# Lambda's scratch in two 8 KB buffers instead of three, and x kept by halves of the features in a GLA / S5 trunk

## The chip, the core and the metric

The kernel runs on one core of one Trainium2 chip. The metric is the device time of one execution in microseconds. A core has five engines that run beside each other and wait for each other by semaphores: TensorE (PE in the profile; PEld are its weight loads), VectorE (DVE), ScalarE (ACT), GpSimd (POOL) and SyncE (SP), which here only issues DMA transfers, one after the other in its queue.

## The reference, cut to what matters

One sequence of 256 tokens with 2048 features goes through two layers: a chunked gated linear attention (GLA), then a complex-diagonal state-space layer (S5). Before each layer the input is modulated by a conditioning vector, after it stands a residual with LayerNorm.

```python
mod = einsum('bd,lde->lbe', silu(c), ada_w) + ada_b          # ada_w: 2 x 2048 x 6144
for i in range(2):
    shift, scale, gate = split(mod[i], 3)
    u = x * (1 + scale) + shift
    h = gla_mixer(u, ...) if i == 0 else s5_mixer(u, ...)
    x = layer_norm(ALPHA * x + (1 + gate) * h, ln_g[i], ln_b[i])
```

The first thing that the GLA layer does with `u` is the product with `gla_w_in` (queries, keys, values, the output gate z). The S5 layer needs numbers that depend on its weights alone. For 256 groups of 64 states:

```python
dt = exp(log_dt);  mag = exp(a_re * dt)
lb = mag * (cos(a_im * dt) + j sin(a_im * dt))               # Lambda
coef = ((lb - 1) * conj(a)) / (a_re**2 + a_im**2)            # scales b
```

The kernel needs `lb`, its powers 1 to 8, and `coef`. It calls this "Lambda's preparation".

## The kernel before, in words

Every large product is made at nearly f32 precision from two parts: a weight block of 256 x 512 is loaded (`wload`, L134, 512 KB, into a ring of four to six buffers), ScalarE makes its rounded part `hi` (`split`, L145), VectorE the remainder `lo` (L146), and TensorE multiplies the activations' parts with them, three matmuls for each pair (`mv_step`, L159, and `st_step`, L171). `hi` and `lo` have three buffers each.

The early part, up to some 360 us, works on values, queries and keys (tiles `v`, `q`, weights `wv`, `wq`). The 2048 features of `u` are taken in four blocks of 2, 2, 4 and 8 slices of 128 (`blocks`, L451), since a slice of `u` exists only when the conditioning (scale, shift) of these features does. `vqk_steps` (L382) gives the 12, 12, 24 and 48 steps of the blocks; the main loop (L801 to L823) runs them in order. Beside the steps run, by a table of steps (`put`, L768):

- the conditioning: `ada_pe` (L243) loads a block `a` of `ada_w` (L254, up to 1 MB), multiplies it on TensorE (`psa`, L275) or on VectorE (tile `row`, L265 to L267) and adds it to `mods`;
- x: `x_load` (L342) loads columns of x for both groups of 128 tokens, `u_tr` (L358) transposes them on TensorE (`psx`, L363), `u_fin` (L366) makes the two parts of `u`. The columns 0 to 255 are loaded ahead of the first step, 256 to 511 at step 0, 512 to 1023 at step 10, 1024 to 2047 at step 30. The last slices of the first half are transposed at step 23, those of the second half at steps 42 to 47;
- Lambda's preparation (`prep_lambda`, L500), a generator that the loop advances once in each step of the third block (steps 24 to 47) and empties after them. It works on tiles of 128 x 128 numbers on VectorE: an exponential by a polynomial (`expx`, L484), a reduction of the angle, two sines on ScalarE, `lr` and `li` (Lambda itself, the first rows of `pw`), `nr`, `den` and `coef` (`crci`), then the powers in three rounds that double their number (m = 1, 2, 4) with a scratch `tm`; last 64 small matmuls (`psl`, L591) on TensorE.

All tiles of up to 8 KB a partition that live longer, among them the blocks `a`, the rows of x, `u`, queries and keys, and Lambda's tiles, come from one pool of 12 buffers, `s8` (L49, `s8t`, L74). A tile gets a buffer when its first instruction comes up and gives it back after its last; an instruction whose buffer is not free waits, and whatever stands behind it in the queue of its engine waits too. In the early part `xrow0` and `xrow1` (one for each 128 tokens, all 2048 features) take two buffers from the first loads to the last transposes. Lambda takes three: `lamst` with 16 rows of 128 numbers, of which `new()` hands out one for each value, `pwr` for the powers, and `pwt` (4 KB used) for the scratch of the power rounds.

Which of the ready instructions stands first in an engine's queue is laid out by a planner when the program is built, from the order of the source, the dependencies and the free buffers. `tc.issue_after` keeps the TensorE and VectorE work of the table behind that of its step.

## Time and profile before

| | |
|---|---|
| median of 3 runs | 1847.61 us |
| lowest and highest run | 1844.9 and 1849.89 us |
| profiled execution, its own time | 1846.54 us |
| its span, first to last instruction | 1844.7 us |
| mean granted TensorE clock | 0.994 |
| TensorE busy | 1795.5 us (97%) |
| VectorE, ScalarE busy | 1422.5 us (77%), 897.4 us (49%) |
| HBM traffic | 432.81 MB read, 14.42 MB written |

A row of the profile names the line of the kernel, the engine, the operation, the tile written and the tiles read (buffer numbers left out), the shape, the count and the times. In the views by time the first number is the start in us from the first instruction, the second the duration; what stands in brackets is the idle time of the engine just before, and what ended it. In the views of waits there follow after the colon the total in us, the number of times and the longest. "issue" is time in which an engine waited for nothing that the profile shows. L136, L145, L146 and L510 are lines of helpers, so that there the tile's name tells what is meant.

### The profile page before, as it was taken

The numbers are of one execution on the slowest core, as the hardware profiler recorded it, in microseconds if no ns is written. First come the engines' busy times: TensorE is split into PE (matmuls) and PEld (weight loads), VectorE is DVE, ScalarE is ACT, GpSimd is POOL, SyncE is SP. The second block draws the span as 40 slices with busy tenths as digits, with TensorE's granted clock in tenths as the row PEclk, the third lists the DMA queues.
The fourth block names the chain that finished last, engine by engine and source line by source line (L and its number), as shares of the span: only waits on it lengthen the run. The fifth ranks groups of instructions, "written<-read, shape, count | busy, mean of one in ns | idle before, by whom it ended". The sixth has DMA issues, their size and how long they took to land.

```text
span 1844.7 us, 33886 instructions
## 1 busy us (share of the span) xinstructions
PE 1795.5 (97%) x13619; PEld 1588.5 (86%) x13619; DVE 1422.5 (77%) x1890; ACT 897.4 (49%) x1252; POOL 72.7 (4%) x78
## 2 busy tenths in 40 slices
PE   7999999999999999999999999999999999999997
PEld 5776897899999888899999999988888888888885
DVE  4877657879989888697899689888677775557556
ACT  5433557556556333654454454545544444444332
POOL 0000000000000000002223200000000000000000
PEclk9999999999999999999999999999999999999999
DMA  9996875889889998465654477899688886668653
GB/s 343 386 333 248 294 244 164 279 261 325 291 286 317 333 353 281 163 220 158 183 151 147 139 214 222 235 246 238 224 276 264 276 271 206 191 189 325 194 184 92
DMA packets 243798, 449.48 MB, mean 244 GB/s; under 512 B 19572, under 2 KB 48942, under 8 KB 242358
## 3 DMA queue, kind: packets, MB, share of 16 engines
q1 hardware_dynamic: 239320, 436.02, 73.9%
q0 software_dynamic: 3552, 10.24, 1.8%
q8 instruction: 107, 1.75, 0.4%
q10 hardware_dynamic: 768, 1.05, 0.2%
q14 instruction: 51, 0.42, 0.1%
HBM read 432.81 MB, written 14.42 MB: 242 GB/s over the span
## 4 chain that ended last, share of the span: by engine, by line
PE 86%; DVE 8%; DMA 3%; ACT 2%; issue 2%; SPq 0%; DVEq 0%; ACTq 0%
PE gl L192 13%; PE gl L193 7%; PE op L168 6%; PE op L167 6%; PE op L169 6%; PE z L182 3%; PE z L180 3%; PE z L181 3%; PE sz L180 3%; PE v L168 3%; PE v L169 3%; PE sz L181 3%; PE sz L182 3%; PE v L167 3%; PE su L180 2%; PE su L182 2%
## 5 line engine op out<-in xcount | busy, mean ns | idle before, releaser
L146 DVE TENSOR_TENSOR logl<-wgl,higl 128x1024 fp32r<-128x1024 f32 x128 | 156.5, 1224 | 115.3 <-ACT higl L145 113.7
L145 ACT CAST higl<-wgl 128x1024 fp32r<-128x1024 f32 x128 | 134.4, 1051 | 172.2 <-PE gl L192 167.9
L192 PE MATMUL gl<-yb,higl 128*128 128x512 f32 x512 | 179.6, 395 | 0.0
L192 PE MATMUL gl<-yp,higl 128*128 128x512 f32 x512 | 179.3, 395 | 0.1
L145 ACT CAST hio<-wo 128x1024 fp32r<-128x1024 f32 x95 | 100.2, 1055 | 155.3 <-PE op L169 127.3
L146 DVE TENSOR_TENSOR loo<-wo,hio 128x1024 fp32r<-128x1024 f32 x95 | 116.2, 1225 | 67.2 <-ACT hio L145 63.7
L315 DVE SCALAR_TENSOR_TENSOR acc<-wa,cs,acc 128x512 f32<-128x512 f32 x217 | 162.2, 748 | 4.8 <-DMA wa<-in_ada_w 2.1
L180 PE MATMUL su<-u1h,hisu 128*128 128x256 f32 x512 | 153.5, 301 | 1.9 <-DVE vv L1108 1.9
L180 PE MATMUL sz<-u1h,hisz 128*128 128x256 f32 x512 | 149.7, 292 | 1.2 <-ACT zs L1290 1.2
L180 PE MATMUL z<-u0h,hiz 128*128 128x256 f32 x512 | 148.7, 290 | 0.0
L182 PE MATMUL su<-u1h,losu 128*128 128x256 f32 x512 | 145.7, 286 | 0.4 <-DVE losu L146 0.4
L181 PE MATMUL su<-u1l,hisu 128*128 128x256 f32 x512 | 145.8, 285 | 0.0
L182 PE MATMUL z<-u0h,loz 128*128 128x256 f32 x512 | 144.9, 283 | 0.6 <-DVE loz L146 0.6
L182 PE MATMUL sz<-u1h,losz 128*128 128x256 f32 x512 | 144.9, 283 | 0.0
L181 PE MATMUL sz<-u1l,hisz 128*128 128x256 f32 x512 | 144.7, 283 | 0.0
L181 PE MATMUL z<-u0l,hiz 128*128 128x256 f32 x512 | 144.7, 283 | 0.0
L193 PE MATMUL gl<-yb,logl 128*128 128x256 f32 x512 | 143.4, 280 | 0.0
L193 PE MATMUL gl<-yp,logl 128*128 128x256 f32 x512 | 142.0, 280 | 0.0
L145 ACT CAST hisz<-wsz 128x1024 fp32r<-128x1024 f32 x64 | 66.9, 1051 | 107.2 <-PE sz L181 55.1
L192 PEld LDWEIGHTS gl<-yb,higl 128*128 128x128 f32 x512 | 96.0, 188 | 22.6
L192 PEld LDWEIGHTS gl<-yp,higl 128*128 128x128 f32 x512 | 95.8, 188 | 22.6 <-issue 0.6
L145 ACT CAST hisu<-wsu 128x1024 fp32r<-128x1024 f32 x64 | 66.7, 1050 | 95.1 <-PE su L181 70.6
(322 smaller groups left out, 5019.8 us busy)
## 6 DMA issues: line engine op xcount, KB each, us to landing
wgl<-in_s_w_glu SPq DMA_DIRECT2D x128, 512.0 KB, 4.7
wa<-in_ada_w SPq DMA_DIRECT2D x116, 512.0 KB, 5.1
wv<-in_gla_w_in SPq DMA_DIRECT2D x64, 512.0 KB, 6.1
wz<-in_gla_w_in SPq DMA_DIRECT2D x64, 512.0 KB, 5.2
wsu<-in_s_w_in SPq DMA_DIRECT2D x64, 512.0 KB, 3.7
wsz<-in_s_w_in SPq DMA_DIRECT2D x64, 512.0 KB, 4.3
wo<-in_s_w_out SPq DMA_DIRECT2D x64, 512.0 KB, 4.5
a<-in_ada_w SPq DMA_DIRECT2D x31, 1024.0 KB, 10.7
```

The costliest lines, as they stand in the source:

```text
L145: S.copy(hi, w)
L146: last_lo[0] = V.tensor_tensor(lo, w, hi.bitcast(F32), op=ALU.subtract).ins
L167: PE.matmul(banks[tt], lhsT=uh, rhs=hi[:, kk, :], start=(k == first), stop=False)
L168: PE.matmul(banks[tt], lhsT=uh, rhs=lo[:, kk, :], start=False, stop=False)
L169: last_mm[0] = PE.matmul(banks[tt], lhsT=ul, rhs=hi[:, kk, :], start=False, stop=(k == last)).ins
L180: PE.matmul(o, lhsT=wh, rhs=u.hi(k), start=(k == first), stop=False)
L181: PE.matmul(o, lhsT=wh, rhs=u.lo(k), start=False, stop=False)
L182: last_mm[0] = PE.matmul(o, lhsT=wl, rhs=u.hi(k), start=False, stop=(k == last)).ins
L192: PE.matmul(banks[f], lhsT=hi[:, kk, fs], rhs=u.both(k), start=(k == 0), stop=False)
L193: PE.matmul(banks[f][:, :T], lhsT=lo[:, kk, fs], rhs=u.hi(k), start=False, stop=(k == last))
L315: V.scalar_tensor_tensor(acc[0], w[:, kk, :], cs[:, k:k + 1], acc[0], op0=ALU.mult, op1=ALU.add)
```

## The change

x is kept in two tiles by halves of the features, 1024 for both token groups each; the second tile is asked for only when its columns are loaded, at step 30. In Lambda's preparation `pwt` goes, and its scratch lies in the rows 8 to 15 of `lamst`; the rows 0 to 6 serve several values in turn. `lamst` is so in use until the last power round.

| row of `lamst` | values, in turn |
|---|---|
| 0, 1 | `ar`, `ai` |
| 2 | `ag`, `cosm` |
| 3 | `mg`, `den` |
| 4 | `th`, `sn`, `t1` |
| 5 | `nn`, `sh`, `t2` |
| 6 | `r`, `nr` |

No arithmetic changes, and the number and shape of the transfers, transposes and VectorE instructions stay.

```diff
-    xr = []
+    xr = {}
     def x_load(c0, c1):
-        if not xr:
-            xr.extend([s8t(f"xrow{i}", [D]) for i in range(2)])
+        h = c0 // 1024
+        if h not in xr:
+            xr[h] = s8t(f"xrow{h}", [2, 1024])
         for tt in range(2):
-            dma(xr[tt][:, c0:c1], x[0, tt * P:(tt + 1) * P, c0:c1])
+            dma(xr[h][:, tt, c0 - 1024 * h:c1 - 1024 * h], x[0, tt * P:(tt + 1) * P, c0:c1])
...
-                PE.transpose(ps[:, kk * T + tt * P:kk * T + (tt + 1) * P], xr[tt][:, k * P:(k + 1) * P], ident)
+                PE.transpose(ps[:, kk * T + tt * P:kk * T + (tt + 1) * P], xr[k // 8][:, tt, k % 8 * P:(k % 8 + 1) * P], ident)
...
     def prep_lambda():
         st = s8t("lamst", [16, 128])
         pw = s8t("pwr", [8, 2, 128])
-        n_ = [0]
-        def new():
-            n_[0] += 1
-            return st[:, n_[0] - 1, :]
+        row = [st[:, i, :] for i in range(7)]
+        tm = st[:, 8:16, :].rearrange("g (a m) p -> g a m p", a=2)
...
-        ar, ai = new(), new()
+        ar, ai = row[0], row[1]
...
-        ag, mg, th = new(), new(), new()
+        ag, mg, th = row[2], row[3], row[4]
...
-        nn, r = new(), new()
+        nn, r = row[5], row[6]
...
-        sn, sh = new(), new()
+        sn, sh = row[4], row[5]
...
-        cosm = new()
+        cosm = row[2]
...
-        nr, den, t1, t2 = new(), new(), new(), new()
+        nr, den, t1, t2 = row[6], row[3], row[4], row[5]
...
-        tm = s8t("pwt", [2, 4, 128])
         for m in (1, 2, 4):
```

## The prediction

> **What bounds the kernel now.** I read the page first, then the windows of the stage in which the touched buffers live, then who waits for whom there, and last the timelines of VectorE, TensorE and the SP queue.

> ```profile
> span 1844.7 us, 33886 instructions
> PE 1795.5 (97%) x13619; PEld 1588.5 (86%) x13619; DVE 1422.5 (77%) x1890; ACT 897.4 (49%) x1252; POOL 72.7 (4%) x78
> PE 86%; DVE 8%; DMA 3%; ACT 2%; issue 2%; SPq 0%; DVEq 0%; ACTq 0%
> ```

> TensorE is busy 1795.5 of 1844.7 us: 49.2 us are idle in the whole program. None of its instructions is touched in number or shape, so a gain can only be a part of those 49.2 us, and of them only the part that falls where the change acts. The next view cuts the early stages; columns are the busy time of PE, weight loads, DVE, ACT and POOL, the granted clock, the DMA share and GB/s.

> ```profile
> 20.00:105.00 85.00, 80.69 (x475) 66.01 (x475) 65.19 (x100) 40.58 (x63) 0.00 (x0) 0.96 1.05 374
> 105.00:150.00 45.00, 43.45 (x230) 30.24 (x230) 33.97 (x87) 15.12 (x20) 0.00 (x0) 1.00 0.88 312
> 150.00:168.00 18.00, 14.07 (x125) 9.10 (x124) 17.61 (x38) 3.70 (x7) 0.00 (x0) 1.00 0.40 130
> 168.00:206.00 38.00, 38.00 (x308) 32.55 (x306) 24.55 (x43) 15.71 (x23) 0.00 (x0) 1.00 0.89 319
> 206.00:230.00 24.00, 22.14 (x183) 21.23 (x182) 15.18 (x20) 17.30 (x22) 4.04 (x4) 1.00 0.94 304
> ```

> The limits differ by stage. From 150 to 168 us VectorE is full (17.61 of 18.00), DMA is nearly empty (0.40) and PE loses 3.93 us; from 168 to 206 us PE loses nothing. The waits of PE and of the SP queue in this stretch:

> ```profile
> PE v L168 <- DVE lov L146: 3.8, 2, 1.9
> PE v L167 <- ACT hiv L145: 1.6, 1, 1.6
> PE pspw L610 <- ACT pd L603: 1.0, 1, 1.0
> PE pspw L610 <- ACT lc L612: 0.8, 2, 0.4
> SPq L254 <- PE psa L275: 29.4, 6, 9.3
> SPq L254 <- DVE crci L510: 9.7, 1, 9.7
> ```

> PE waits 7.2 us from 105 to 230 us, always for VectorE or ScalarE. The SP queue stands 39.1 us at L254, the load of a conditioning block `a`, until a buffer is given back: six times by the matmuls `psa` that read an older block, once by the end of Lambda's scratch `lamst`. That is the shortage the change relieves, and no PE wait of this list ends on a DMA.

> **The change, part by part.** *Buffers.* There are 12. Four are held in this stage by `u0h0`, `u0l0`, `qk0`, `qk1`; before, both `xrow` buffers are held until the last token transposes. Afterwards one half of x is enough until step 30, none is held between steps 23 and 30, and `pwt` needs none. The SP queue in the stage:

> ```profile
> 123.23 0.93 SPq L346 DMA_DIRECT2D xrow<-in_x  x2
> 133.66 0.37 SPq L254 DMA_DIRECT2D a<-in_ada_w  x1
> 135.47 2.25 SPq L136 DMA_DIRECT2D wv<-in_gla_w_in  x2
> 144.80 0.37 SPq L254 DMA_DIRECT2D a<-in_ada_w  x1
> 145.26 0.46 SPq L136 DMA_DIRECT2D wq<-in_gla_w_in  x1
> 155.48 0.37 SPq L254 DMA_DIRECT2D a<-in_ada_w  x1
> 155.90 1.01 SPq L136 DMA_DIRECT2D wq<-in_gla_w_in  x2
> 166.33 0.37 SPq L254 DMA_DIRECT2D a<-in_ada_w  x1
> ```

> With one or two buffers more, the `a` loads at 133.66, 144.80 and 155.48 can go right behind the load ahead of them: the second at about 137.8 (the end of the row at 135.47), the third as soon as an older block has been read, some us after that, and the first weight of the two at 155.90 follows at once. So most of the 39.1 us leave the SP queue. For the end of the kernel I take 0 from this. What hides the late loads now is the weights' lead: the rows at 151 to 168 us show PE short of casts and remainders that VectorE makes, not of data, and from 168 to 206 us PE is never idle. Bounds: from 0 down to the 7.2 us of all PE waits above; 0 is nearer, as none of the four rows ends on a DMA.

> *x by halves.* Eight loads remain eight, of the same bytes; 32 transposes remain 32 of one shape; the two loads at 123.23 wait for a new buffer instead of writing columns of an old one. Their data is read here:

> ```profile
> 181.91 0.60 PE L363 MATMUL psx<-ident,xrow 128*128 128x128 f32 x4
> 169.19 0.69 DVE L401 TENSOR_TENSOR vbig<-vbig,v 128x512 f32<-128x512 f32 x1 [1.35 <-PE v L169]
> ```

> 58 us later. Were the buffer late by the longest wait seen (9.3 us), the weights queued behind it would move by as much, which is the collision rival below; I take 0. `lamst` is now held to the end of the power loop (about 166.7 us instead of just before the load at 155.48 that got it), but with the freed buffers nobody asks for that one before the load that now leaves at 166.33: 0.

> *Rows used in turn.* Seven rows serve fourteen values. For most the order was forced by data already: `cosm`, `sn`, `sh`, `nr`, `t2` each overwrite a value whose last reader ran before their own inputs exist. One case differs: `den`, from `ar` and `ai` alone, now lies in the row of `mg`, and its helper `t1` in the row of `sn`; both are read by `lr` and `li`. VectorE's queue is laid out by a planner, and before the change it pulled those four instructions far forward:

> ```profile
> 121.99 0.81 DVE L510 TENSOR_TENSOR lamst<-lamst 128x128 f32<-128x128 f32 x3
> 122.84 0.95 DVE L557 RECIPROCAL lamst<-lamst 128x128 f32<-128x128 f32 x1
> 125.03 0.16 DVE L241 SCALAR_TENSOR_TENSOR mods<-psmod,abT 128x4 f32<-128x4 f32 x1 [1.23 <-PE psmod L236]
> ```

> They ran at 122 us, ahead of everything else of Lambda, in a pause: the next instruction waited 1.23 us for PE, so taking them away there gains nothing. They now come behind `lr` and `li`, here:

> ```profile
> 152.37 0.49 DVE L510 TENSOR_TENSOR pwr<-lamst 128x128 f32<-128x128 f32 x2
> 152.78 0.22 DVE L553 TENSOR_SCALAR lamst<-pwr 128x128 f32<-128x128 f32 x1
> 155.34 0.29 DVE L510 TENSOR_TENSOR pwt<-pwr 128x128 f32<-128x128 f32 x1
> 155.54 1.22 DVE L146 TENSOR_TENSOR lov<-wv,hiv 128x1024 fp32r<-128x1024 f32 x1
> 160.49 1.22 DVE L146 TENSOR_TENSOR lov<-wv,hiv 128x1024 fp32r<-128x1024 f32 x1
> 161.63 1.29 DVE L510 TENSOR_TENSOR pwt<-pwr 128x512 f32<-128x512 f32 x2
> 166.01 0.69 DVE L510 TENSOR_TENSOR pwr<-pwt 128x512 f32<-128x512 f32 x1
> 156.81 0.50 PE L168 MATMUL v<-lov,u0h 128*128 128x512 f32 x1 [1.89 <-DVE lov L146]
> 161.76 0.50 PE L168 MATMUL v<-lov,u0h 128*128 128x512 f32 x1 [1.94 <-DVE lov L146]
> 166.77 0.58 PE L591 MATMUL psl<-ident,pwr 128*32 128x32 f32 x32
> ```

> This is the stretch in which VectorE has no pause and PE waits for it twice. The four instructions took from 121.99 to 123.79, 1.80 us; back to back, each starts some 0.08 us before the end of the one ahead (0.29 long, 0.20 from 155.34 to 155.54), so they lengthen a full queue by about **1.7 us**. Queued behind them: the remainders `lov` at 155.54 and 160.49, for which PE waits, and the last power row at 166.01 + 0.69 = 166.70, at which PE arrives at 166.77. All three are on the path, so the 1.7 us are paid once. Bounds: 0, if the planner sets them behind the remainders and into the pause of 1.35 us at 169.19 (its row is above); and 1.7 us plus the power loop's tail, 166.70 - 161.63 = 5.1 us, if PE has to stand for it. I take 1.7, since the queue was laid out with Lambda ahead of the remainders.

> [...]

> **Sum.** 0 (buffers) + 0 (x) + 1.7 (`den`) on the profiled execution's own 1846.54 us (span 1844.7 and 1.8 around it) gives **1848.2 us**. The median of the runs, 1847.61, lies 1.1 above that execution, and the same step on it would read 1849.3. A measurement of this kernel tells about 0.3%, 5.5 us, from no change: my forecast is no measurable change.

> **The rivals.**

> *The buffers were the limit after all* (faster). For it: 39.1 us of SP waits, and DMA at 0.40 of its time where PE loses most. Against it: those PE waits end on VectorE and ScalarE. If late loads stand behind them, all four rows fall: 1846.5 - 7.2 = 1839.3 us. [...]

> *PE stands at `psl`* (slower). The 64 matmuls `psl` keep their place in PE's queue whatever happens to Lambda. If the planner lets the four late instructions push the power loop's tail behind the remainders, PE reaches `psl` and waits for that tail: 1.7 + 5.1 = 6.8 us, 1853.3 us. It decides as soon as the last power row is written after PE has done all that is queued ahead; before, that margin was 166.77 - 166.70 = 0.07 us, which speaks for it. Against: the other order needs a new plan, and PE's queue would be planned anew too.

> *The four instructions vanish in a pause* (nothing). They are placed behind the remainders, or PE's two waits swallow them: 1846.5 us. The same time results if the change does not do what it says, and the loads stay bound by weight buffers.

> *Loads collide* (a little slower). Loads pulled forward compete with weights:

> ```profile
> a<-in_ada_w SPq DMA_DIRECT2D x11, 1024.0 KB, 9.3
> wv<-in_gla_w_in SPq DMA_DIRECT2D x10, 512.0 KB, 7.7
> 154.51 1.05 ACT L145 CAST hiv<-wv 128x1024 fp32r<-128x1024 f32 x1 [2.07 <-PE v L169]
> ```

> At the 374 GB/s of a full DMA window 1 MB takes 2.8 us. The last weight `wv` (issued by 137.7, landed some 7.7 us later at 145.4) is cast at 154.51: 9.1 us to spare. Four loads ahead of it cost 11.2 us, 2.1 more than it has: 1846.5 + 1.7 + 2.1 = 1850.3 us. It bites from the fourth load on.

> **How the numbers follow.** Forecast 0.36, nothing 0.20, collision 0.08: together 0.64 within 0.3%. Buffers the limit 0.17, faster by over 0.3%. PE at `psl` 0.19, slower by over 0.3%. The range takes the slower case in whole and the faster one down to its foot, 1839.0 to 1855.0 us: beyond it are plans that I cannot work out, some 2 in 10. The forecast's own range is 1845 to 1851.

> **What would show it.** Right: the reciprocal at L557 runs after `lr` and `li`, past 150 us, not at 122; the waits of L254 for `psa` and `crci` shrink to under 15 us together, yet PE's waits from 105 to 230 us stay between 7 and 11 us; DMA has more than 0.40 from 150 to 168 us. Wrong: PE's waits for `lov` go away (buffers), `psl` gets a wait of its own (the slower rival), `hiv` ends a wait on a DMA (collision), or a difference of over 3 us arises past 230 us, where nothing is touched.

## The result and the profile after

| | before | after |
|---|---|---|
| median of 22 runs each, side by side | 1846.61 us | 1852.63 us |
| lowest and highest run | 1843.68 and 1851.98 us | 1848.35 and 1857.09 us |
| profiled execution, its own time | 1846.54 us | 1852.82 us |
| mean granted TensorE clock of that execution | 0.994 | 0.991 |

The ratio is 1.0028, with a 95% interval of 1.002 to 1.0036: about 5 us slower (the medians lie 6.0 us apart). The 0.3% that I called the limit lies inside the interval, no change lies outside it. The forecast was 1848.2 us; its wide range of 1839 to 1855 us holds the time, the forecast's own range of 1845 to 1851 us does not.

The page of after begins so; PE does the same 13619 matmuls, but is busy 3.4 us longer, and its idle time grows from 49.2 to 52.1 us:

```profile
span 1851.0 us, 33889 instructions
PE 1798.9 (97%) x13619; PEld 1589.1 (86%) x13619; DVE 1421.6 (77%) x1890; ACT 898.8 (49%) x1252; POOL 75.4 (4%) x78
```

The windows of the early stages of after, columns as before (us; PE, PEld, DVE, ACT, POOL; granted clock, DMA share, GB/s):

```profile
105.00:150.00 45.00, 43.45 (x235) 30.45 (x235) 33.42 (x87) 15.35 (x22) 0.00 (x0) 1.00 0.97 345
150.00:168.00 18.00, 11.75 (x41) 8.33 (x39) 15.65 (x38) 4.10 (x4) 0.00 (x0) 0.85 0.43 148
168.00:206.00 38.00, 38.00 (x330) 29.29 (x332) 22.86 (x37) 12.23 (x18) 0.00 (x0) 0.94 0.76 258
206.00:230.00 24.00, 22.92 (x187) 21.41 (x187) 13.06 (x24) 14.96 (x20) 2.89 (x3) 1.00 0.69 211
```

From 150 to 168 us PE is busy 11.75 us, not 14.07, and the clock, 1.00 throughout before, is 0.85 here and 0.94 in the next stage. The waits of PE from 105 to 230 us, and below them those of the SP queue at the `a` loads from 105 to 200 us (after the colon: us in total, times, longest):

```profile
PE v L168 <- DVE lov L146: 6.1, 2, 3.5
PE v L167 <- ACT hiv L145: 1.6, 1, 1.6
PE pspw L609 <- ACT lc L611: 0.4, 1, 0.4
```

and, of the SP queue:

```profile
SPq L254 <- PE psa L275: 15.1, 2, 13.5
SPq L254 <- PE v L169: 0.6, 1, 0.6
SPq L136 <- DVE lov L146: 24.4, 8, 6.2
```

The SP queue's 39.1 us for `psa` and `crci` have become 15.1 us, and the wait for `crci` is gone: the change does what it says. But the queue now stands longer at the weight loads (L136), 24.4 us for buffers that the remainders `lov` read (all its waits of this stretch sum to 73.5 us in both kernels), where the same view of before has:

```profile
SPq L136 <- DVE lov L146: 10.1, 4, 5.1
```

PE gains nothing by it; its two waits for `lov` rise from 3.8 to 6.1 us. The timelines show where, VectorE's first (start and duration in us):

```profile
153.58 0.49 DVE L510 TENSOR_TENSOR pwr<-lamst 128x128 f32<-128x128 f32 x2
155.12 0.95 DVE L557 RECIPROCAL lamst<-lamst 128x128 f32<-128x128 f32 x1
158.34 1.23 DVE L146 TENSOR_TENSOR lov<-wv,hiv 128x1024 fp32r<-128x1024 f32 x1
162.16 0.69 DVE L403 TENSOR_TENSOR vbig<-vbig,v 128x512 f32<-128x512 f32 x1 [0.67 <-PE v L169]
163.56 0.69 DVE L403 TENSOR_TENSOR vbig<-vbig,v 128x512 f32<-128x512 f32 x1 [0.38 <-PE v L169]
164.17 1.29 DVE L510 TENSOR_TENSOR lamst<-pwr 128x512 f32<-128x512 f32 x2
165.37 1.22 DVE L146 TENSOR_TENSOR lov<-wv,hiv 128x1024 fp32r<-128x1024 f32 x1
```

PE in the same time:

```profile
159.63 0.79 PE L168 MATMUL v<-lov,u0h 128*128 128x512 f32 x1 [3.49 <-DVE lov L146]
160.65 0.63 PE L167 MATMUL v<-hiv,u0h 128*128 128x512 f32 x1
166.64 0.80 PE L168 MATMUL v<-lov,u0h 128*128 128x512 f32 x1 [2.66 <-DVE lov L146]
177.71 0.28 PE L180 MATMUL q<-u0h,hiq 128*128 128x256 f32 x1
```

The reciprocal runs at 155.12 us behind `lr` and `li`, as forecast. The first wait grows by 3.49 - 1.89 = 1.60 us, about the 1.7 us of the four instructions. The second grows too, by 0.72 us. And behind each wait the matmuls are slow: 0.63 us long, where before they took 0.39. The first product with queries starts at 177.71 us; before, it started at 170.36. Of these 7.35 us, 1.2 were there already when `lr` and `li` ran (153.58 us against 152.37); about 6.1 arise here.

One more cut of the windows shows why. The clock's changes in the record lie on a comb with teeth 3.41 us apart (in after at 159.12, 162.53, 165.95 and, two teeth on, 172.77 us); cut on that comb, after reads:

```profile
155.71:159.12 3.41, 0.43 (x2) 0.00 (x1) 3.41 (x14) 1.05 (x1) 0.00 (x0) 1.00 0.96 362
159.12:162.53 3.41, 2.90 (x7) 2.32 (x8) 2.67 (x7) 0.00 (x0) 0.00 (x0) 0.50 0.49 145
162.53:165.95 3.42, 1.46 (x7) 0.85 (x5) 3.04 (x6) 1.05 (x1) 0.00 (x0) 1.00 0.02 8
165.95:169.36 3.41, 2.72 (x36) 1.86 (x37) 3.41 (x5) 0.00 (x0) 0.00 (x0) 0.50 0.00 0
169.36:172.77 3.41, 3.41 (x11) 1.86 (x13) 1.91 (x3) 0.00 (x0) 0.00 (x0) 0.50 0.02 5
```

In the interval behind one in which PE was mostly idle (0.43 of 3.41 us busy, 1.46 of 3.42), TensorE is here granted half its clock; a third interval at half clock follows one at half clock in which PE was busy for 2.72 us. The price can be read from PE's rows: from the end of the first wait to the first product with queries it takes 18.1 us (159.63 to 177.71), before 13.6 us (156.81 to 170.36). Of the 4.5 us more, 0.7 are the second wait and 3.8 the slow matmuls. With the first wait's 1.6 us these are the 6.1 us. The kernel before has the same two waits, shorter. These are its two emptiest intervals of this stretch, and the clock stays full in them and behind them:

```profile
153.18:156.58 3.40, 1.75 (x8) 1.13 (x6) 3.40 (x14) 1.05 (x1) 0.00 (x0) 1.00 0.02 2
160.01:163.42 3.41, 1.66 (x7) 1.39 (x8) 3.41 (x6) 0.45 (x1) 0.00 (x0) 1.00 0.83 295
```

So the theory was, ahead of the experiments: **A**, the late `den` makes PE wait longer for `lov`, and the longer waits cost clock. Its rivals: **B**, x by halves or the buffers it frees; **C**, the longer hold of `lamst` with the third buffer gone; and that the clock has nothing to do with the waits.

### The profile page after: what moved, and what is told of

Read it like the earlier page. It is cut to its first block, busy times and chain, and to the rows that moved or that the text cites. A ratio compares the mean times of both kernels' runs of the same rounds, so it can differ in the third digit from the quotient of the medians.

```text
span 1851.0 us, 33889 instructions
## 1 busy us (share of the span) xinstructions
PE 1798.9 (97%) x13619; PEld 1589.1 (86%) x13619; DVE 1421.6 (77%) x1890; ACT 898.8 (49%) x1252; POOL 75.4 (4%) x78
## 3 DMA queue, kind: packets, MB, share of 16 engines
q8 instruction: 107, 1.75, 0.4%
q10 hardware_dynamic: 768, 1.05, 0.2%
## 4 chain that ended last, share of the span: by engine, by line
PE 82%; DVE 10%; DMA 3%; issue 2%; ACT 2%; SPq 1%; DVEq 0%; ACTq 0%
PE gl L192 13%; PE gl L193 7%; PE op L168 6%; PE op L169 6%; PE op L167 6%; PE z L182 3%; PE z L180 3%; PE z L181 3%; PE v L168 3%; PE v L169 3%; PE v L167 3%; PE sz L180 2%; PE sz L182 2%; PE sz L181 2%; PE su L180 2%
## 5 line engine op out<-in xcount | busy, mean ns | idle before, releaser
L146 DVE TENSOR_TENSOR logl<-wgl,higl 128x1024 fp32r<-128x1024 f32 x128 | 156.5, 1224 | 114.4 <-ACT higl L145 112.5
L145 ACT CAST higl<-wgl 128x1024 fp32r<-128x1024 f32 x128 | 134.6, 1052 | 172.6 <-PE gl L192 163.4
L145 ACT CAST hio<-wo 128x1024 fp32r<-128x1024 f32 x95 | 100.3, 1056 | 154.1 <-PE op L169 130.5
L146 DVE TENSOR_TENSOR loo<-wo,hio 128x1024 fp32r<-128x1024 f32 x95 | 116.6, 1229 | 66.8 <-ACT hio L145 64.8
L145 ACT CAST hisz<-wsz 128x1024 fp32r<-128x1024 f32 x64 | 67.0, 1051 | 103.2 <-PE sz L181 55.3
L168 PE MATMUL v<-lov,u0h 128*128 128x512 f32 x256 | 104.4, 409 | 10.0 <-DVE lov L146 9.9
## 6 DMA issues: line engine op xcount, KB each, us to landing
wgl<-in_s_w_glu SPq DMA_DIRECT2D x128, 512.0 KB, 4.8
wa<-in_ada_w SPq DMA_DIRECT2D x116, 512.0 KB, 4.8
wv<-in_gla_w_in SPq DMA_DIRECT2D x64, 512.0 KB, 5.7
wz<-in_gla_w_in SPq DMA_DIRECT2D x64, 512.0 KB, 5.3
wsu<-in_s_w_in SPq DMA_DIRECT2D x64, 512.0 KB, 3.7
wsz<-in_s_w_in SPq DMA_DIRECT2D x64, 512.0 KB, 3.8
wo<-in_s_w_out SPq DMA_DIRECT2D x64, 512.0 KB, 4.5
a<-in_ada_w SPq DMA_DIRECT2D x31, 1024.0 KB, 10.8
```

The source lines that it names most:

```text
L145: S.copy(hi, w)
L146: last_lo[0] = V.tensor_tensor(lo, w, hi.bitcast(F32), op=ALU.subtract).ins
L168: PE.matmul(banks[tt], lhsT=uh, rhs=lo[:, kk, :], start=False, stop=False)
```

## The experiments

All were timed against the kernel before on the same chip. The table gives means. The four groups of one chip each (e1 to e4; e5 to e8; e9 and e10; e11 and e12) had runs of before beside them, with means of 1847.3, 1847.6, 1847.0 and 1847.2 us. "Clock" is one minus the mean granted clock (noted to 0.001 for each run), times the span, averaged over the runs (its standard error is 0.3 to 0.6 us in each row); "rest" is the time less that. "Clock" counts all the time at half clock, whether TensorE worked in it or not.

| kernel | runs | mean us | ratio to before, 95% interval | clock, us | rest, us |
|---|---|---|---|---|---|
| before (the runs beside the first four) | 35 | 1847.3 | | 14.2 | 1833.1 |
| after | 22 | 1852.2 | 1.0028 (1.002 to 1.0036) | 16.4 | 1835.8 |
| e1: after, `den` in rows of its own | 12 | 1847.4 | 0.9997 (0.9985 to 1.0009) | 13.7 | 1833.7 |
| e2: before, `den` in shared rows | 12 | 1851.2 | 1.0024 (1.0011 to 1.0036) | 16.8 | 1834.4 |
| e3: before, x by halves of the features | 12 | 1846.4 | 0.999 (0.9975 to 1.0005) | 13.4 | 1833.1 |
| e4: before, Lambda's part of the change | 12 | 1853.2 | 1.0032 (1.002 to 1.0045) | 17.0 | 1836.3 |
| e7: after, PE's waits filled | 12 | 1848.0 | 1.0001 (0.999 to 1.0012) | 12.2 | 1835.8 |
| e8: after, `den` computed twice | 12 | 1848.7 | 1.0007 (0.9996 to 1.0017) | 14.3 | 1834.3 |
| e10: before, PE's waits filled | 11 | 1847.3 | 0.9999 (0.9986 to 1.0012) | 12.9 | 1834.4 |
| e5: e1, Lambda six steps earlier | 12 | 1843.0 | 0.9977 (0.9965 to 0.9988) | 12.7 | 1830.3 |
| e6: after, Lambda six steps earlier | 9 | 1841.9 | 0.9968 (0.9955 to 0.998) | 12.3 | 1829.7 |
| e9: before, Lambda six steps earlier | 12 | 1845.1 | 0.9993 (0.9982 to 1.0005) | 13.1 | 1832.0 |
| e11: e6 again, beside e12 | 11 | 1844.4 | 0.9989 (0.9978 to 0.9999) | 13.1 | 1831.4 |
| e12: e9 again, beside e11 | 11 | 1844.8 | 0.9987 (0.9975 to 0.9999) | 12.6 | 1832.2 |

### Which part of the change

e1, on after:

```diff
-        row = [st[:, i, :] for i in range(7)]
+        row = [st[:, i, :] for i in range(8)]
...
-        nr, den, t1, t2 = row[6], row[3], row[4], row[5]
+        nr, den, t1, t2 = row[6], row[7], row[4], row[5]
+        dh = tm[:, 1, 3, :]
...
-        tt(t1, ai, ai, ALU.mult)
-        tt(den, den, t1, ALU.add)
+        tt(dh, ai, ai, ALU.mult)
+        tt(den, den, dh, ALU.add)
```

> The kernel after, but `den` lies in the free row 7 of `lamst` and its helper in row 15 (the last row of the power loop's scratch, not used before m = 4); two buffers, x by halves, the rest as in after. Theory A (late `den`): the four instructions run at about 122 us again, PE's waits for `lov` in 150-170 us fall from 6.2 to about 3.8 us, no half-clock interval in 150-175 us, time as before, about 1846.6 us (1845 to 1848.5). Theory B (x by halves or the buffers it frees is the cause): as after, about 1852.6 us, whatever `den` does. Theory C (the longer hold of `lamst` and the missing third buffer): as after, about 1852.6 us.

e2, on before:

```diff
-        nr, den, t1, t2 = new(), new(), new(), new()
+        nr, den, t1, t2 = new(), mg, sn, new()
```

> The kernel before, but `den` in the row of `mg` and `t1` in the row of `sn`; three buffers, all other rows their own, x by tokens. Theory A: reciprocal at about 155 us behind `lr` and `li`, PE's waits for `lov` in 150-170 us about 6 us, half-clock intervals of 3 to 10 us behind them, time as after, about 1852.6 us (1850.5 to 1854). Theory B: as before, 1846.6 us, as x is as before. Theory C: as before, 1846.6 us, as the three buffers are as before; the late `den` alone then costs at most the 1.7 us of its four instructions, 1848.3.

e3 is before with only the `x_load` and `u_tr` part of the change, e4 before with only its `prep_lambda`.

> The kernel before with only x kept by halves of the features; Lambda's preparation as before, in three buffers with rows of their own. Theory A: as before, 1846.6 us (1845 to 1848.5), the reciprocal at about 122 us, the SP queue's waits for `psa` shorter than 29.4 us all the same. Theory B: as after, about 1852.6 us. Theory C: as before, 1846.6 us.

> The kernel before with only Lambda's preparation as in after (two buffers, rows in turn); x kept by halves of the tokens. Theory A: as after, about 1852.6 us (1850.5 to 1854), reciprocal at about 155 us, waits for `lov` about 6 us, half-clock intervals behind them. Theory B: as before, 1846.6 us. Theory C: as after, 1852.6 us.

The two kernels with shared rows are slow, the two without are not, whatever x and the buffers do. One line of e2 (three buffers, x by tokens) already makes 3.9 us of loss, where after has 4.9; the intervals overlap. And e1, which has both freed buffers, x by halves and the longer hold of `lamst`, is as fast as before. B and C fall. In e1 the reciprocal (VectorE's timeline) and the two waits of PE (its waits from 105 to 230 us) are back where before has them:

```profile
123.54 0.95 DVE L558 RECIPROCAL lamst<-lamst 128x128 f32<-128x128 f32 x1
```

```profile
PE v L168 <- DVE lov L146: 3.7, 2, 1.9
```

and in the same view of waits e2 is as after:

```profile
PE v L168 <- DVE lov L146: 6.1, 2, 3.5
```

I had missed one thing of e1: there should have been no half-clock interval, and its profiled execution has two, with waits no longer than those of before:

```profile
154.37:157.79 3.42, 1.54 (x7) 1.00 (x6) 3.38 (x13) 1.05 (x1) 0.00 (x0) 1.00 1.01 369
157.79:161.20 3.41, 3.41 (x9) 2.64 (x9) 2.45 (x6) 0.00 (x0) 0.00 (x0) 0.50 0.68 217
161.20:164.61 3.41, 1.63 (x7) 1.01 (x7) 2.92 (x6) 1.05 (x1) 0.00 (x0) 1.00 0.00 0
164.61:168.03 3.42, 3.42 (x10) 2.63 (x9) 3.38 (x5) 0.00 (x0) 0.00 (x0) 0.50 0.00 0
```

The comb lies otherwise against the same waits and catches 1.54 and 1.63 busy us, where it caught 1.75 and 1.66 in before. So by these four intervals a wait of 1.9 us stands at the edge: whether it costs clock seems to depend on where the comb falls.

### Whether the clock follows the waits

e7, on after; in the steps of weights v63 and v72 twelve matmuls are put behind the first matmul with `hiv`, in `mv_step`. The weight tile `zp` is zero, so they add nothing. The heart of the edit, cut to it (the matmuls with `lov` are kept behind the last of them):

```diff
...
+                if fill and tt == 0 and kk == 0:
+                    for _ in range(fill):
+                        with tc.issue_after(m_):
+                            m_ = PE.matmul(banks[tt], lhsT=zp, rhs=hi[:, kk, :], start=False, stop=False).ins
...
```

> The kernel after, plus 24 extra matmuls on PE, twelve behind the first matmul with `hiv` of weight v63 and twelve behind that of v72, ahead of the first matmuls with `lov`: 128x512 with a weight tile of zeros, so that they add nothing to the bank. At 0.227 us each at full clock they take 2.7 us inside each of the two waits (3.49 and 2.66 us) and add no wait. Clock theory (PE left idle for most of a 3.4 us interval runs the next at half clock): the granted clock stays 1.0 from 150 to 180 us, and the two waits for `lov` end as early as in after; the mean falls by the clock's part of the loss, 2 to 3 us, to about 1849.5 us (after was 1852.2 in the mean), though PE has 24 matmuls more. Rival (the half clock has nothing to do with the idle time, or the late `lov` alone is the loss): no gain or, where the fill makes PE late, up to 1 us slower, 1852 to 1853.

The 24 matmuls more make the kernel 4.3 us faster than after (1848.0 against 1852.2). All of it is clock: the rest is 1835.8 us in both, the clock falls from 16.4 to 12.2 us. The comb's intervals in e7:

```profile
155.25:158.66 3.41, 3.41 (x17) 2.83 (x16) 3.41 (x15) 1.06 (x1) 0.00 (x0) 1.00 1.04 384
158.66:162.07 3.41, 2.64 (x12) 1.87 (x11) 3.34 (x8) 0.00 (x0) 0.00 (x0) 1.00 0.42 108
162.07:165.49 3.42, 3.42 (x16) 2.65 (x15) 3.42 (x6) 1.05 (x1) 0.00 (x0) 1.00 0.25 95
```

This shows cause, not company: PE was kept busy with work worth nothing, and the half clock went. VectorE's timeline of e7 also explains the second wait:

```profile
158.66 1.22 DVE L146 TENSOR_TENSOR lov<-wv,hiv 128x1024 fp32r<-128x1024 f32 x1
161.73 0.68 DVE L411 TENSOR_TENSOR vbig<-vbig,v 128x512 f32<-128x512 f32 x1
163.26 1.29 DVE L518 TENSOR_TENSOR lamst<-pwr 128x512 f32<-128x512 f32 x2
164.46 1.22 DVE L146 TENSOR_TENSOR lov<-wv,hiv 128x1024 fp32r<-128x1024 f32 x1
```

From one `lov` to the next it takes 5.80 us; in after 7.03 us, since there VectorE itself waited 0.67 and 0.38 us for PE at half clock, with the next `lov` behind; in before 4.95 us, since there the pair of 1.29 us stood behind the second `lov`, not ahead of it. So the new order puts the next `lov` 0.85 us later, and the slow clock another 1.2 us. But PE's own matmuls between its two waits take longer at half clock, too: 4.35 us in after against 3.01 in before. The two about cancel, and the wait itself grows by the order alone. The profile of e4 bears this out: its clock was full between the two waits, and they are about as long as in after:

```profile
159.24 0.50 PE L168 MATMUL v<-lov,u0h 128*128 128x512 f32 x1 [3.49 <-DVE lov L146]
165.04 0.79 PE L168 MATMUL v<-lov,u0h 128*128 128x512 f32 x1 [2.78 <-DVE lov L146]
```

e10 fills before's two waits in the same way, with seven matmuls each:

> The kernel before, plus seven extra matmuls with a weight tile of zeros (7 x 0.227 = 1.6 us) inside each of PE's two waits of 1.9 us for `lov`. Clock theory: the kernel before stands at the edge, its two waits leave an interval 0.45 to 0.53 busy, so that in some executions they cost half-clock intervals; the fill takes these away: mean clock loss 12 to 13 us in place of 14.1, mean time 1845.5 to 1846.5, and no half-clock interval from 150 to 175 us. Rival (waits of 1.9 us never cost clock): no change, 1847.4 us in the mean.

This did not settle it. The clock's part was 12.9 us (14.0 in the runs of before beside it), a difference of less than two of its standard errors; no half-clock interval lies in the stretch, but none does in the profile of before either. And the time did not fall, 1847.3 against 1847.0 us: the waits, fill included, got longer.

```profile
PE v L176 <- DVE lov L146: 1.8, 2, 1.3
```

That is the same view of e10's waits: 1.8 us, and 14 x 0.227 = 3.2 us of fill make 5.0 us, where before waits 3.8. The fill shifted VectorE's queue: the pair of 1.29 us now stands ahead of the second `lov`, as in after, and from one `lov` to the next it takes 6.13 us, where before takes 4.95. So whether waits of 1.9 us cost before any clock in the mean stays open.

### Twice the cost

e8, on after: the four lines of `den` written a second time behind the first, the same values again.

> The kernel after, with the four instructions of `den` written twice behind each other (the second time writes the same values again), so 1.7 us more on VectorE behind `lr` and `li`. Theory A with my price: PE's waits for `lov` grow by 1.7 us at the first of the two remainders, 6.2 to about 7.9 us, and the time by 1.7 us plus up to one more half-clock interval (1.7): about 1854 to 1856 us in the mean. Rival (it was only the new order in PE's and VectorE's queues that cost time): no growth, 1852.2.

A miss: not 1.7 us slower than after, but 3.6 us faster (1848.7). Its wait from 105 to 230 us, three rows of VectorE's timeline and two intervals of the comb say why:

```profile
PE v L168 <- DVE lov L146: 5.3, 1, 5.3
```

```profile
159.94 1.22 DVE L146 TENSOR_TENSOR lov<-wv,hiv 128x1024 fp32r<-128x1024 f32 x1
161.41 1.22 DVE L146 TENSOR_TENSOR lov<-wv,hiv 128x1024 fp32r<-128x1024 f32 x1
163.22 1.22 DVE L146 TENSOR_TENSOR lov<-wv,hiv 128x1024 fp32r<-128x1024 f32 x1
```

```profile
157.55:160.97 3.42, 0.00 (x0) 0.00 (x0) 3.42 (x12) 0.00 (x0) 0.00 (x0) 1.00 0.24 93
160.97:164.38 3.41, 3.16 (x8) 2.49 (x9) 3.41 (x7) 0.00 (x0) 0.00 (x0) 0.50 0.50 153
```

The first wait did grow, by 5.34 - 3.49 = 1.85 us, as priced. But the planner laid the queue out anew and put the next two `lov` at 161.41 and 163.22 us, ahead of most of the power loop; the second wait is gone, and one interval at half clock stands where after had three. One wait of 5.3 us was cheaper than two of 3.5 and 2.7. The rival that I set against my price (the order costs, too) has a part in it: VectorE's extra time is paid at the next remainder, and what is paid at the one after depends on the order. My price so holds for the first wait only; the time does not follow the number of late instructions.

### Taking the cause away

e5 (on e1), e6 (on after) and e9 (on before) advance Lambda's preparation from step 18 on, not 24, into the stretch in which VectorE had 11 us free:

```diff
-            if n == 2:
+            if n == 2 or n == 1 and i >= 6:
                 next(lam, None)
```

> The first experiment's kernel (`den` and its helper in rows of their own, otherwise as after), with the generator of Lambda's preparation advanced from the seventh weight step of the second block on, six steps earlier. Theory A (VectorE is full only from 150 to 168 us and has 11 us free from 105 to 150): the waits for `lov` in 150-170 us (3.7 us) go, no wait as long comes up before 150 us, no half-clock interval there; 3.7 us less and up to 2 us of clock: 1842 to 1844 us in the mean, faster than before. Rival (VectorE is short over the whole stretch, so the waits only move): `lov` waits of about the same sum at 115 to 150 us, time 1846 to 1848.

> The kernel after, rows shared as they are, with the generator advanced six steps earlier as in the run beside it. Theory A: the row sharing costs only where VectorE is full, so the time is that of the run beside it within 1 us, 1842 to 1845 us. Rival (the order that the shared rows force costs by itself): 2 us or more slower than the run beside it.

> The kernel before (three buffers, rows of their own, x by tokens) with the generator of Lambda's preparation advanced six weight steps earlier. Theory A (only VectorE's full stretch counts, buffers and x do not): the same gain as with the shared rows and halves of the features, 1842 to 1843.5 us in the mean. Rival (the freed buffers are what the earlier Lambda needs, as its `lamst` and `pwr` are held longer): the SP queue's waits for `psa` grow beyond 39 us and the gain is smaller, 1844.5 us or more.

e5 and e6 are faster than before, and within 1.1 us of each other: the shared rows cost nothing that these runs show once Lambda's chain runs where VectorE has time. The windows of e6 from 105 to 150 and from 150 to 180 us, where VectorE is now busy 41.43 of 45 and 14.49 of 30 us, and PE's waits for `lov` from 105 to 230 us:

```profile
105.00:150.00 45.00, 42.34 (x283) 28.46 (x282) 41.43 (x109) 14.84 (x22) 0.00 (x0) 1.00 0.89 309
150.00:180.00 30.00, 29.89 (x189) 23.62 (x188) 14.49 (x20) 9.98 (x11) 0.00 (x0) 1.00 0.89 324
```

```profile
PE v L168 <- DVE lov L146: 2.5, 2, 2.1
```

The waits for `lov` in the old place are gone; 2.5 us stand at 108 and 142 us. e5's own expectation missed in one point: it has a wait of 2.3 us for `hiv` ahead of 150 us, longer than any that went. In e11 and e12 an interval near 106 us, busy for 0.39 and 0.42, is followed by half clock. So the earlier Lambda, too, can cost clock, at a place of its own. e9 gained less (0.9993, the interval across 1), as its rival had it, but its SP queue did not wait longer for `psa` (26.1 us, not over 39), so that rival's reason was not seen. e11 and e12 set the two side by side on one chip:

> The kernel after with Lambda's preparation six steps earlier, once more, now on the same chip as its counterpart without the change. If the freed buffers are worth nothing even then, the two means lie within 1.5 us of each other, at 1842 to 1845.5 us. If the freed buffers are worth something once VectorE is out of the way, this one is faster by 2 to 3 us, as the separate runs (1841.9 against 1845.1 us) have it.

> The kernel before with Lambda's preparation six steps earlier, once more, on the same chip as the run beside it. Buffers worth nothing: within 1.5 us of it. Buffers worth something: slower than it by 2 to 3 us.

1844.4 and 1844.8 us: no difference beyond the noise (up to some 2 us would not show). The freed buffers show no worth here either. The gain of the kernel with the change over before was 5.7 us in the first comparison (e6) and 2.7 us in the second (e11): its sign is settled, its size is not. Against after it is 7 us or more in both, so the kernel with the change and an earlier Lambda beats both kernels.

## Why the prediction was right or wrong

**Buffers, 0; x by halves, 0.** Right. e1 (0.9997) has both freed buffers, e3 (0.999) that of x, each with the interval across 1, and e11 against e12 repeats it with VectorE out of the way. It fits the reason given, that none of PE's waits in this stage ended on a transfer. The waits of L254 for `psa` and `crci` fell to 15.1 us, where I had set under 15; the weight loads behind them took up the freed time as waits of their own.

**`den`, 1.7 us.** The mechanism was right, and the size at its place too (1.60 us). The step that failed is "all three are on the path, so the 1.7 us are paid once". They are paid once at the first `lov`; the third, the last power row, was never waited for. And the sum lacked two terms. The second wait grew by 0.72 us, from the new order (0.84 us in e4, whose clock was full there). And the clock: 2.2 us in the mean (16.4 against the 14.2 of the 35 runs in the table), 3.8 us in the profiled execution. With 2.7 us in the rest (the two waits, 1.60 + 0.72 = 2.3 us, are most of it) this makes the 4.9 us between those means; against the 22 runs of before beside it, whose clock was not noted run by run, after is 5.2 us slower. The part of the sum that was mis-sized is thus "1.7", which measured 4.9 to 5.2; I had read the clock's 1.00 in that stage as given, not as something which a longer wait takes away. VectorE does 1890 instructions in both kernels; where four of them stand was worth 3.9 us in e2 and this much in after.

**"PE stands at `psl`"** said 1853.3 us, the number nearest to the result, by a mechanism that did not occur: `psl` has no wait, its halves only stand later in PE's queue:

```profile
168.22 0.66 PE L590 MATMUL psl<-ident,pwr 128*32 128x32 f32 x32
174.69 0.46 PE L590 MATMUL psl<-ident,pwr 128*32 128x32 f32 x32
```

The prediction said that `psl` keeps its place in PE's queue whatever happens to Lambda; it did not. A number that fits shows no cause; e1 and e2 do. **"Four instructions vanish in a pause"** fell with the reciprocal at 155.12 us, **"Loads collide"** with `hiv`, whose only wait of PE is the 1.6 us of before, **"Buffers were the limit"** with e1 and e3.

**Chances and signs.** By the ratio the result is within 0.3%, the case that had 0.64, but only by 0.0002; by the medians it is just outside, on the side that had 0.19. That the 0.3% holds it is luck, and that the wide range holds it says little, since that range was drawn around nearly all the rivals; the forecast's own range, 1845 to 1851 us, misses the mean (1852.2) and the median. My chances also add up to 1 without the 2 in 10 that I set beyond the range, so the two statements do not fit. My cases treated "a little slower" as the forecast and "much slower" as a rival; the truth lay between them. DMA from 150 to 168 us rose to 0.43, and PE's waits from 105 to 230 us were 8.1 us, both as forecast. Past 230 us the distance between the two profiled executions changes by less than the 3 us that I had named: it is 7.35 us at the first product with queries, 8.2 at PE's wait near 766 us, 8.7 near 1002 us and 6.3 at the end.

## What to carry to other kernels

Sharing rows between values removes no work, but it ties instructions that were free to run early to the last reader of the row; look at where they ran before, and at how full the engine is where they will run now. A wait on TensorE is to be priced with the clock that it can cost, here 2.2 us in the mean beside 2.3 us of longer waits: cut the windows on the clock's own comb and see whether the emptiest intervals are like the 48 at full clock that half clock followed here, all but one of them busy for less than half of their 3.41 us. And before buffers are freed, see whether a wait on the path ends on a transfer; here none in this stage did, and the freed buffers brought nothing.

## What the hardware showed that was not expected

The comb lay differently in the profiles that are cut on it above (a tooth at 153.18 us in before, 155.71 in after, 154.37 in e1, 155.25 in e7, 157.55 in e8), so waits like those of before and e1 should make a kernel's time scatter. That is argued, not shown: the runs of before have standard deviations of 2.3 to 3.1 us and those of e5, without such waits from 150 to 168 us, 1.0 us, but those of e9, without them too, have 2.6 us.
